# A log-sum-exp scan that is bound by its DMA engines: an opening store, and a part of one tile stored through GpSimd's queue

## Chip, cores, metric

One Trainium2 (trn2) chip, one core. The metric is the time on the device in microseconds (us); lower is better.

## The reference

```python
# x: (8, 4096, 2048) float32; a running log-sum-exp along axis 1
out[:, 0, :] = x[:, 0, :]
for t in range(1, S):
    mx = np.maximum(out[:, t - 1, :], x[:, t, :])
    out[:, t, :] = mx + np.log(np.exp(out[:, t - 1, :] - mx) + np.exp(x[:, t, :] - mx))
```

## The kernel before

The kernel takes 64 tiles of 128 partitions x 4 rows x 2048 columns (4 MB each), in six buffers. SP loads a tile; ScalarE (ACT) takes Exp; VectorE (DVE) adds the four rows of each partition; TensorE makes the sums over the partitions before; VectorE adds them; ACT takes Ln and stores the tile. Every load and store covers all 128 partitions. The parts that matter here:

```python
def parts(n):                                   # pieces in which a tile is stored
    m = 2 if n == NT - 1 else 1
    return [slice(k * R // m, (k + 1) * R // m) for k in range(m)]
...
for rows, c in ((slice(0, 2), top), (slice(2, R), loaded[0])):   # first tile, ahead of the block
    c(nc.sync.dma_start(out=ti[0][:, rows, :], in_=x_v[0][:, rows, :]), 16)
...
# SP: loads
for n in range(1, NT):
    i = n % NI
    if n >= NI:
        sp.wait_ge(stored[i].s, n // NI * 16)   # the store that frees the buffer
    loaded[i](sp.dma_start(out=ti[i][:], in_=x_v[n]), 16)
...
# ACT, in ln(n), second half of the columns
stored[n % NI](act.dma_start(out=o_v[n][:, rows, :], in_=t[:, rows, :]), 16)
...
# after the block
for c in stored:
    nc.sync.wait_ge(c.s, c.n)
```

The softmax here doesn't subtract the row's maximum and nothing guards it: scores larger than these inputs give would overflow.

Of the kernel before, what the change touches and what calls it, by code (L numbers as in the profile page):

```python
# [8 lines left out]
@with_exitstack  # L9
def kernel(  # L10
    ctx: ExitStack,
    tc: tile.TileContext,
    x: bass.AP,
    out: bass.AP,
):











    nc = tc.nc
    f32 = mybir.dt.float32
    ACT = mybir.ActivationFunctionType
    nc.scalar.preload_act_table_set("natural_log_exp_and_others")  # L30

    B, S, D = x.shape
    P = 128
    R = 4
    NI = 6
    FD = 512
    HALF = D // 2
    NBLK = S // (P * R)
    NT = B * NBLK
    assert D == 4 * FD  # L40

    pool = ctx.enter_context(tc.tile_pool(name="io", bufs=1))
    psum = ctx.enter_context(tc.tile_pool(name="ps", bufs=1, space=bass.MemoryType.PSUM))
    before = pool.tile([P, P], f32, name="before", tag="before")
    last = pool.tile([P, P], f32, name="last", tag="last")
    ti = [pool.tile([P, R, D], f32, name=f"ti{i}", tag=f"ti{i}") for i in range(NI)]
    ps = [psum.tile([P, D], f32, name=f"ps{i}", tag=f"ps{i}") for i in range(2)]

    x_v = x.rearrange("b (k p r) d -> (b k) p r d", p=P, r=R)
    o_v = out.rearrange("b (k p r) d -> (b k) p r d", p=P, r=R)  # L50
    half = [slice(h * HALF, (h + 1) * HALF) for h in range(2)]

    def parts(n):

        m = 2 if n == NT - 1 else 1
        return [slice(k * R // m, (k + 1) * R // m) for k in range(m)]

    class Count:


        def __init__(self, name):
            self.s, self.n = tc.alloc_semaphore(name), 0

        def __call__(self, inst, by=1):
            inst.then_inc(self.s, by)
            self.n += by
            return self.n

    with tc.tile_critical():  # L69
        def counts(name, n):  # L70
            return [Count(f"{name}{i}") for i in range(n)]

        ones, shaped, logs, top, chain = (
            Count(s) for s in ("ones", "shaped", "logs", "top", "chain")
        )

        loaded, stored = counts("loaded", NI), counts("stored", NI)
        exps, sums, ahead, joined, carried = (
            counts(s, 2) for s in ("exps", "sums", "ahead", "joined", "carried")
        )  # L80


        for rows, c in ((slice(0, 2), top), (slice(2, R), loaded[0])):
            c(nc.sync.dma_start(out=ti[0][:, rows, :], in_=x_v[0][:, rows, :]), 16)  # L84

        with nc.Block() as block:  # L86

            @block.gpsimd
            def _(g):
                ones(g.memset(before[:], 1.0))  # L90
                ones(g.memset(last[:], 1.0))  # L91
                g.wait_ge(ones.s, ones.n)

                shaped(g.affine_select(  # L94
                    out=before[:], in_=before[:], compare_op=mybir.AluOpType.is_ge, fill=0.0,
                    base=-1, pattern=[[1, P]], channel_multiplier=-1,
                ))

                shaped(g.affine_select(  # L99
                    out=last[:], in_=last[:], compare_op=mybir.AluOpType.is_ge, fill=0.0,  # L100
                    base=-(P - 1), pattern=[[0, P]], channel_multiplier=1,
                ))

            @block.sync
            def _(sp):
                for n in range(1, NT):
                    i = n % NI
                    if n >= NI:
                        sp.wait_ge(stored[i].s, n // NI * 16)
                    loaded[i](sp.dma_start(out=ti[i][:], in_=x_v[n]), 16)  # L110

            @block.scalar
            def _(act):
                def exp(n):
                    t = ti[n % NI]
                    lo = 0
                    if n == 0:
                        lo = 2
                        act.activation(t[:, :lo], t[:, :lo], ACT.Exp)._wait_ge(top.s, 16)  # L119
                    for h in range(2):  # L120
                        a = act.activation(t[:, lo:, half[h]], t[:, lo:, half[h]], ACT.Exp)  # L121
                        if h == 0:
                            a._wait_ge(loaded[n % NI].s, (n // NI + 1) * 16)
                        exps[h](a)

                def ln(n):
                    t = ti[n % NI]
                    for h in range(2):
                        for rows in parts(n) if h else [slice(0, R)]:
                            logs(act.activation(  # L130
                                t[:, rows, half[h]], t[:, rows, half[h]], ACT.Ln
                            )._wait_ge(carried[h].s, n + 1))
                            if h:
                                act.wait_ge(logs.s, logs.n)
                                stored[n % NI](act.dma_start(  # L135
                                    out=o_v[n][:, rows, :], in_=t[:, rows, :]
                                ), 16)

                exp(0)
                for n in range(NT):  # L140
                    if n + 1 < NT:
                        exp(n + 1)
                    ln(n)

            @block.tensor
            def _(pe):
                def carry(n, h):

                    if n % NBLK == NBLK - 1:
                        pe.wait_ge(joined[h].s, n + 1)  # L150
                        pe.sem_inc(carried[h].s, 1)  # L151
                        return
                    for c in range(2 * h, 2 * h + 2):
                        sl = slice(c * FD, (c + 1) * FD)
                        m = pe.matmul(  # L155
                            ps[(n + 1) % 2][:, sl], last[:], ti[n % NI][:, R - 1, sl],
                            start=True, stop=False, skip_group_check=True,
                        )
                        if c == 2 * h:
                            m._wait_ge(joined[h].s, n + 1)  # L160
                    carried[h](m)

                def triangle(n, h):
                    for c in range(2 * h, 2 * h + 2):
                        sl = slice(c * FD, (c + 1) * FD)
                        m = pe.matmul(  # L166
                            ps[n % 2][:, sl], before[:], ti[n % NI][:, R - 1, sl],
                            start=n % NBLK == 0, stop=True, skip_group_check=True,
                        )
                        if c == 2 * h:  # L170
                            m._wait_ge(sums[h].s, n + 1)
                    ahead[h](m)

                pe.wait_ge(shaped.s, shaped.n)
                for n in range(NT):
                    for h in range(2):
                        triangle(n, h)
                    for h in range(2):
                        carry(n, h)

            @block.vector
            def _(dve):
                def local(n, h):
                    t, cols = ti[n % NI], half[h]
                    for r in range(1, R):
                        a = dve.tensor_add(t[:, r, cols], t[:, r - 1, cols], t[:, r, cols])  # L186
                        if r == 1:
                            a._wait_ge(exps[h].s, n + 1)
                        else:
                            a._wait_ge(chain.s, chain.n)  # L190
                        (chain if r < R - 1 else sums[h])(a)

                def join(n, h):
                    t, cols = ti[n % NI], half[h]
                    joined[h](dve.tensor_add(  # L195
                        t[:, :, cols], t[:, :, cols],
                        ps[n % 2][:, cols].unsqueeze(1).to_broadcast([P, R, HALF]),
                    )._wait_ge(ahead[h].s, n + 1))

                for n in range(NT):  # L200
                    for h in range(2):
                        local(n, h)
                    for h in range(2):
                        join(n, h)

        for c in stored:
            nc.sync.wait_ge(c.s, c.n)


# [28 lines left out]
```

## Time and profile before

| | before |
|---|---|
| time, median of six runs | 1250.51 us (1250.36 to 1250.60) |
| bytes moved | 268.44 MB in, 268.44 MB out |
| mean rate over the span | 430 GB/s |
| busy: VectorE, ScalarE, TensorE | 82%, 73%, 52% |
| last landing of a store | 1246.77 us after the start |
| end of the span | 1248.83 us |

The kernel is bound by its DMA engines; the lines that show it stand in the prediction. A useful habit for such a kernel is to look at the sixteen landings of one transfer, one per engine: the last of them ends the transfer. For the last store before the change they lie between 1243.30 and 1246.77 us, and their mean is 1244.67.

### The profile page before, as it was taken

The page shows a single profiled execution, that of the slowest core. Times are in us where ns is not written, and L with a number is a line of the kernel's source. Part 1 is how long each engine was busy: PE and PEld are TensorE (multiplying, and loading weights), DVE is VectorE, ACT ScalarE, POOL GpSimd, SP SyncE. Part 2 cuts the span into 40 slices and gives each one's busy share as a digit, 9 for nine tenths or more (in the row PEclk, how much of TensorE's full clock was granted, in tenths as well). Part 3 has the DMA queues.
Part 4 walks back from the last instruction along what each step waited for, and adds up shares of the span by engine and source line. Part 5 has one row for each costly group of instructions (what it writes and reads, how often), then busy time and mean ns, then how long its engine had stood idle before and what let it go on. Part 6 is the DMA issues. An engine that isn't in the chain of part 4 may idle for free.

```text
span 1248.8 us, 2916 instructions
## 1 busy us (share of the span) xinstructions
PE 645.1 (52%) x960; PEld 213.4 (17%) x960; DVE 1022.3 (82%) x512; ACT 907.5 (73%) x259; POOL 1.1 (0%) x8
## 2 busy tenths in 40 slices
PE   2655456553556444655465544555545564455551
PEld 0211112111112111211111111111111121111110
DVE  5999978778787787887878878778787787877873
ACT  5987866867768677686776866867768677686773
POOL 0000000000000000000000000000000000000000
PEclk9899788787887868777678786787767878778776
DMA  9999999999999999999999999999999999999998
GB/s 403 420 431 431 430 437 436 427 434 432 437 435 426 435 432 437 433 428 435 431 437 433 430 435 430 437 431 432 436 430 436 432 432 435 431 436 432 431 435 361
DMA packets 18735, 537.06 MB, mean 430 GB/s; under 512 B 2080, under 2 KB 2080, under 8 KB 2080
## 3 DMA queue, kind: packets, MB, share of 16 engines
q1 hardware_dynamic: 9360, 268.44, 49.9%
q10 hardware_dynamic: 9360, 268.44, 49.8%
q8 instruction: 7, 0.11, 0.0%
q14 instruction: 8, 0.07, 0.0%
HBM read 268.44 MB, written 268.44 MB: 430 GB/s over the span
## 4 chain that ended last, share of the span: by engine, by line
DMA 80%; ACT 14%; DVE 4%; PE 1%; DVEq 0%; issue 0%; SPq 0%; ACTq 0%; PEldq 0%
DMA out_dram<-ti 41%; DMA ti<-in_x_dram 38%; ACT ti L130 7%; ACT ti L121 7%; DVE ti L195 2%; DVE ti L186 1%; PE ps L166 1%; DVEq L86 0%; PE ps L155 0%; SPq L84 0%; ACTq L135 0%; PEldq L151 0%; SPq L233 0%; SPq L69 0%
## 5 line engine op out<-in xcount | busy, mean ns | idle before, releaser
L121 ACT ACTIVATE ti<-ti 128x4096 f32<-128x4096 f32 (+1 forms) x128 | 452.5, 3582 | 308.2 <-DMA ti<-in_x_dram 306.0
L186 DVE TENSOR_TENSOR ti<-ti 128x1024 f32<-128x1024 f32 x384 | 464.6, 1224 | 196.6 <-ACT ti L121 187.9
L195 DVE TENSOR_TENSOR ti<-ti,ps 128x4096 f32<-128x4096 f32 x128 | 560.0, 4416 | 9.0 <-PE ps L166 8.8
L166 PE MATMUL ps<-ti,before 128*128 128x512 f32 x512 | 373.2, 879 | 347.1 <-DVE ti L186 347.0
L130 ACT ACTIVATE ti<-ti 128x4096 f32<-128x4096 f32 x129 | 455.8, 3576 | 9.5 <-PE ps L155 6.6
L155 PE MATMUL ps<-ti,last 128*128 128x512 f32 x448 | 271.9, 738 | 228.9 <-DVE ti L195 228.9
L166 PEld LDWEIGHTS ps<-ti,before 128*128 128x128 f32 x512 | 127.5, 276 | 607.4 <-DVE ti L186 503.2
L155 PEld LDWEIGHTS ps<-ti,last 128*128 128x128 f32 x448 | 85.9, 212 | 399.5 <-DVE ti L195 332.8
L119 ACT ACTIVATE ti<-ti 128x4096 f32<-128x4096 f32 x1 | 3.6, 3616 | 6.3 <-DMA ti<-in_x_dram 6.3
L30 ACT ACT_TABLE_LOAD x1 | 1.3, 1283 | 0.8 <-PEq L222 0.8
L94 POOL TENSOR_SCALAR_AFFINE_SELECT before<-before 128x128 f32<-128x128 f32 x1 | 0.3, 292 | 0.1
L99 POOL TENSOR_SCALAR_AFFINE_SELECT last<-last 128x128 f32<-128x128 f32 x1 | 0.3, 292 | 0.0
L90 POOL MEMSET before<- 128x128 f32 x1 | 0.2, 204 | 0.5 <-SPq L69 0.5
L91 POOL MEMSET last<- 128x128 f32 x1 | 0.2, 204 | 0.0
L222 POOL MEMSET const-bfloat16-1.0<- 128x1 bf16 x1 | 0.1, 101 | 0.0
L222 POOL MEMSET const-uint8-127<- 128x1 uint8 x1 | 0.1, 101 | 0.0
L222 POOL MEMSET const-float32-0.0<- 128x1 f32 x1 | 0.1, 98 | 0.3 <-issue 0.3
L222 POOL MEMSET const-float32-1.0<- 128x1 f32 x1 | 0.1, 98 | 0.0
## 6 DMA issues: line engine op xcount, KB each, us to landing
ti<-in_x_dram SPq DMA_DIRECT2D x63, 4096.0 KB, 38.5
out_dram<-ti ACTq DMA_DIRECT2D x63, 4096.0 KB, 44.0
ti<-in_x_dram SPq DMA_DIRECT2D x2, 2048.0 KB, 9.6
out_dram<-ti ACTq DMA_DIRECT2D x2, 2048.0 KB, 13.2
```

The lines of the kernel that those rows point to most:

```text
L30: nc.scalar.preload_act_table_set("natural_log_exp_and_others")
L90: ones(g.memset(before[:], 1.0))
L94: shaped(g.affine_select(out=before[:], in_=before[:], compare_op=mybir.AluOpType.is_ge, fill=0.0, base=-1, pattern=[[1, P]], channel_mult ...
L99: shaped(g.affine_select(out=last[:], in_=last[:], compare_op=mybir.AluOpType.is_ge, fill=0.0, base=-(P - 1), pattern=[[0, P]], channel_mu ...
L119: act.activation(t[:, :lo], t[:, :lo], ACT.Exp)._wait_ge(top.s, 16)
L121: a = act.activation(t[:, lo:, half[h]], t[:, lo:, half[h]], ACT.Exp)
L130: logs(act.activation(t[:, rows, half[h]], t[:, rows, half[h]], ACT.Ln)._wait_ge(carried[h].s, n + 1))
L155: m = pe.matmul(ps[(n + 1) % 2][:, sl], last[:], ti[n % NI][:, R - 1, sl], start=True, stop=False, skip_group_check=True,)
L166: m = pe.matmul(ps[n % 2][:, sl], before[:], ti[n % NI][:, R - 1, sl], start=n % NBLK == 0, stop=True, skip_group_check=True,)
L186: a = dve.tensor_add(t[:, r, cols], t[:, r - 1, cols], t[:, r, cols])
L195: joined[h](dve.tensor_add(t[:, :, cols], t[:, :, cols], ps[n % 2][:, cols].unsqueeze(1).to_broadcast([P, R, HALF]),)._wait_ge(ahead[h].s, ...
L222: nc = _bacc.Bacc("TRN2", target_bir_lowering=False, num_devices=1)
```

## The change

The intent: the store queue is opened at the start, so that the first real store doesn't pay for it; the engines are to end together, by having the fifth DMA engine skip a part of tile 40; and the end of the program is to be shorter. Cut to its core:

```diff
+        if n == NT - 1:
+            return [slice(0, 1), slice(1, 2), slice(2, R)]
+        return [slice(0, 2), slice(2, R)] if n == VIA else [slice(0, R)]
+    VIA, PASS = 40, 120
 ...
-    with tc.tile_critical():
+    with tc.tile_critical(no_gpsimd_drain=True):
 ...
+    # ACT, first thing: the opening store
+    warm(act.dma_start(out=o_v[0][0:16, 0, 0:1], in_=nc.const_aps.tensor(0.0, [16, 1], f32)), 16)
 ...
+    own = slice(0, P)
+    if n == VIA and rows.start == 0:
+        share.add(act)
+        own = slice(PASS, P)                    # ACT keeps 8 partitions
-    stored[n % NI](act.dma_start(out=o_v[n][:, rows, :], in_=t[:, rows, :]), 16)
+    stored[n % NI](act.dma_start(out=o_v[n][own, rows, :], in_=t[own, rows, :]), 16)
 ...
+    # SP, before load 46
+    if n - NI == VIA:
+        sp.wait_ge(passed.s, 16)
 ...
+    # GpSimd
+    aimed(g.dma_start(out=spare[0:5, 16:32], in_=spare[0:5, 0:16]), 16)   # "aims" the next one
+    aimed.now(g)
+    share.now(g)
+    rows = parts(VIA)[0]                        # rows 0 and 1
+    passed(g.dma_start(out=o_v[VIA][0:PASS, rows, :], in_=ti[VIA % NI][0:PASS, rows, :]), 16)
+    passed.now(g)
+    # then it sets most semaphores back by hand; SP does so for the stores, inside the block
-        for c in stored:
-            nc.sync.wait_ge(c.s, c.n)
```

More of the change, by code (lines that the diff above doesn't have):

```diff
@@ L45 @@
     last = pool.tile([P, P], f32, name="last", tag="last")
+    spare = pool.tile([8, 32], f32, name="spare", tag="spare")
     ti = [pool.tile([P, R, D], f32, name=f"ti{i}", tag=f"ti{i}") for i in range(NI)]
@@ L53, in parts, with __init__ @@
     def parts(n):
-        m = 2 if n == NT - 1 else 1
-        return [slice(k * R // m, (k + 1) * R // m) for k in range(m)]
+        if n == NT - 1:
+            return [slice(0, 1), slice(1, 2), slice(2, R)]
+        return [slice(0, 2), slice(2, R)] if n == VIA else [slice(0, R)]
+    VIA, PASS = 40, 120
+    every = []
     class Count:
-        def __init__(self, name):
-            self.s, self.n = tc.alloc_semaphore(name), 0
+        def __init__(self, name, alloc=nc.alloc_semaphore):
+            self.s, self.n = alloc(name), 0
+            if alloc == nc.alloc_semaphore:
+                every.append(self)
         def __call__(self, inst, by=1):
@@ L66, in __call__, with add, now, settle @@
             self.n += by
-            return self.n
-    with tc.tile_critical():
+        def add(self, engine):
+            engine.sem_inc(self.s, 1)
+            self.n += 1
+        def now(self, engine):
+            engine.wait_ge(self.s, self.n)
+        def settle(self, engine):
+            if self.n:
+                engine.add_instruction(mybir.InstEventSemaphore(
+                    name=f"I-{nc.next_id()}", engine=engine.engine, ins=[], outs=[],
+                    sync_info=mybir.SyncInfo(
+                        on_wait=[mybir.SyncWait(
+                            sync_type="semaphore", id=self.s.num, ant_name=self.s.name,
+                            wait_mode="sem-ge-imm", wait_value=self.n,
+                        )],
+                        on_update=[mybir.SyncUpdate(
+                            sync_type="semaphore", id=self.s.num, ant_name=self.s.name,
+                            update_mode="sem-sub-imm", update_value=self.n,
+                        )],
+                    ),
+                ))
+    with tc.tile_critical(no_gpsimd_drain=True):
         def counts(name, n):
             return [Count(f"{name}{i}") for i in range(n)]
-        ones, shaped, logs, top, chain = (
-            Count(s) for s in ("ones", "shaped", "logs", "top", "chain")
+        ones, shaped, logs, top, chain, warm, share, over = (
+            Count(s) for s in ("ones", "shaped", "logs", "top", "chain", "warm", "share", "over")
         )
+        aimed, passed = (Count(s, tc.alloc_semaphore) for s in ("aimed", "passed"))
         loaded, stored = counts("loaded", NI), counts("stored", NI)
@@ L80 @@
         )
-        for rows, c in ((slice(0, 2), top), (slice(2, R), loaded[0])):
-            c(nc.sync.dma_start(out=ti[0][:, rows, :], in_=x_v[0][:, rows, :]), 16)
-        with nc.Block() as block:
-            @block.gpsimd
-            def _(g):
-                ones(g.memset(before[:], 1.0))
-                ones(g.memset(last[:], 1.0))
-                g.wait_ge(ones.s, ones.n)
-                shaped(g.affine_select(
-                    out=before[:], in_=before[:], compare_op=mybir.AluOpType.is_ge, fill=0.0,
-                    base=-1, pattern=[[1, P]], channel_multiplier=-1,
-                ))
-                shaped(g.affine_select(
-                    out=last[:], in_=last[:], compare_op=mybir.AluOpType.is_ge, fill=0.0,
-                    base=-(P - 1), pattern=[[0, P]], channel_multiplier=1,
-                ))
-            @block.sync
-            def _(sp):
-                for n in range(1, NT):
-                    i = n % NI
-                    if n >= NI:
-                        sp.wait_ge(stored[i].s, n // NI * 16)
-                    loaded[i](sp.dma_start(out=ti[i][:], in_=x_v[n]), 16)
+        with nc.Block(no_gpsimd_drain=True) as block:
             @block.scalar
             def _(act):
+                with nc.allow_non_contiguous_dma(reason="one element per DMA engine"):
+                    warm(act.dma_start(
+                        out=o_v[0][0:16, 0, 0:1], in_=nc.const_aps.tensor(0.0, [16, 1], f32)
+                    ), 16)
                 def exp(n):
@@ L133, in ln @@
                             if h:
-                                act.wait_ge(logs.s, logs.n)
+                                logs.now(act)
+                                own = slice(0, P)
+                                if n == VIA and rows.start == 0:
+                                    share.add(act)
+                                    own = slice(PASS, P)
                                 stored[n % NI](act.dma_start(
-                                    out=o_v[n][:, rows, :], in_=t[:, rows, :]
+                                    out=o_v[n][own, rows, :], in_=t[own, rows, :]
                                 ), 16)
                 exp(0)
+                warm.now(act)
                 for n in range(NT):
@@ L143, in _ @@
                     ln(n)
+                over.add(act)
+            @block.sync
+            def _(sp):
+                for rows, c in ((slice(0, 2), top), (slice(2, R), loaded[0])):
+                    c(sp.dma_start(out=ti[0][:, rows, :], in_=x_v[0][:, rows, :]), 16)
+                for n in range(1, NT):
+                    i = n % NI
+                    if n >= NI:
+                        sp.wait_ge(stored[i].s, 16 * sum(len(parts(m)) for m in range(i, n, NI)))
+                        if n - NI == VIA:
+                            sp.wait_ge(passed.s, 16)
+                    loaded[i](sp.dma_start(out=ti[i][:], in_=x_v[n]), 16)
+                for n in range(NT - NI, NT):
+                    stored[n % NI].settle(sp)
             @block.tensor
@@ L150, in carry @@
                         pe.wait_ge(joined[h].s, n + 1)
-                        pe.sem_inc(carried[h].s, 1)
+                        carried[h].add(pe)
                         return
@@ L172, in triangle @@
                     ahead[h](m)
-                pe.wait_ge(shaped.s, shaped.n)
+                pe.wait_ge(shaped.s, 2)
                 for n in range(NT):
@@ L179, in _ @@
                         carry(n, h)
+                over.add(pe)
             @block.vector
@@ L204, in _ @@
                         join(n, h)
-        for c in stored:
-            nc.sync.wait_ge(c.s, c.n)
+                over.add(dve)
+            @block.gpsimd
+            def _(g):
+                ones(g.memset(before[:], 1.0))
+                ones(g.memset(last[:], 1.0))
+                ones.now(g)
+                shaped(g.affine_select(
+                    out=before[:], in_=before[:], compare_op=mybir.AluOpType.is_ge, fill=0.0,
+                    base=-1, pattern=[[1, P]], channel_multiplier=-1,
+                ))
+                shaped(g.affine_select(
+                    out=last[:], in_=last[:], compare_op=mybir.AluOpType.is_ge, fill=0.0,
+                    base=-(P - 1), pattern=[[0, P]], channel_multiplier=1,
+                ))
+                ones(g.memset(spare[:], 0.0))
+                ones.now(g)
+                aimed(g.dma_start(out=spare[0:5, 16:32], in_=spare[0:5, 0:16]), 16)
+                aimed.now(g)
+                share.now(g)
+                rows = parts(VIA)[0]
+                passed(g.dma_start(
+                    out=o_v[VIA][0:PASS, rows, :], in_=ti[VIA % NI][0:PASS, rows, :]
+                ), 16)
+                passed.now(g)
+                over.now(g)
+                for c in every:
+                    if c not in stored:
+                        c.settle(g)
 _INS = ['x']
```

## The prediction

> **What bounds the kernel now.** I read the page from the top: the slices of the span, then the queues, then the chain.
>
> ```profile
> DMA  9999999999999999999999999999999999999998
> GB/s 403 420 431 431 430 437 436 427 434 432 437 435 426 435 432 437 433 428 435 431 437 433 430 435 430 437 431 432 436 430 436 432 432 435 431 436 432 431 435 361
> ...
> q1 hardware_dynamic: 9360, 268.44, 49.9%
> q10 hardware_dynamic: 9360, 268.44, 49.8%
> q8 instruction: 7, 0.11, 0.0%
> q14 instruction: 8, 0.07, 0.0%
> ...
> DMA 80%; ACT 14%; DVE 4%; PE 1%; DVEq 0%; issue 0%; SPq 0%; ACTq 0%; PEldq 0%
> ```
>
> The 16 DMA engines are full from the second slice to the last but one; the two data queues take 49.9 + 49.8% of their time. The program must move 537 MB whatever it does, and the change moves the same bytes. So only four things can shorten it: the start (403 and 420 GB/s in the first two slices), the last slice (361), an uneven load of the 16 engines, and what lies outside the transfers. The waits say that compute never starves the queues:
>
> ```profile
> SPq L110 <- DMA out_dram<-ti: 1145.3, 58, 58.2
> ...
> ACT ti L121 <- DMA ti<-in_x_dram: 306.0, 59, 6.0
> ```
>
> A load waits for the store that frees its buffer, and is issued 19.35 us apart (the distance of two loads in the trace). It lands 38.5 us later, so about one full load is always queued ahead of it, and the engines never see an empty ring. An engine that is late therefore stays late, and the slowest of the 16 sets the end. Stretches show it:
>
> ```profile
> 0.00:31.00 31.00, 8.64 (x12) 2.99 (x12) 15.46 (x8) 16.65 (x7) 1.08 (x8) 1.00 0.96 405
> 31.00:62.00 31.00, 20.26 (x32) 6.67 (x32) 30.51 (x17) 28.03 (x9) 0.00 (x0) 0.83 1.00 421
> ...
> 1235.00:1247.00 12.00, 0.00 (x0) 0.00 (x0) 0.00 (x0) 0.00 (x0) 0.00 (x0) 0.50 0.77 328
> ```
>
> The last two columns are DMA share and GB/s. From 1235 on no compute engine works any more. The last landing is at 1246.77, the span's end at 1248.83, and the measured time 1250.37.
>
> **The sixteen engines one by one.** The trace names no engine for a packet, but an engine starts its next packet 3 ns before the last one's modelled end, and each takes eight packets of every transfer and then one 4-byte semaphore write. With those two rules the packets fall into 16 chains of exactly 520 packets per queue. The ends of the last data packets: seven chains at 1242.96 to 1243.5, seven at 1244.4 to 1244.85, and **two stragglers at 1246.30 and 1246.29**. Why they differ:
> - One 16 KB fetch of instructions on q8 costs its chain about 1.35 us (the fetch, 0.95, and some 0.39 more on the packet after it). The seven fetches fall on seven chains: most of the middle group.
> - Straggler A gets four of the 8 KB fetches on q14 (at 103, 404, 715, 1025 us). Each takes 0.309 and lengthens the next packet by 0.54: 4 x 0.85 = 3.4 us, which is its lag over the fastest chain (3.34). No q8 fetch falls on it.
> - Straggler B has no fetch at all. Its 32 KB packets take 1213 ns like everybody's until about 390 us; after that some 260 of them take about 5 to 20 ns more, 2.7 us in all. It is also the chain that starts last (2.79 us against 2.04).
>
> [...]q1 and q10 alternate packet by packet.
>
> **The change part by part.**
> 1. *Relief of the fifth engine.* Two rows of tile 40 are 16 KB per partition. Before, each engine stores 8 x 16 KB = 128 KB of them. After, fifteen engines store 8 partitions each, the fifth none, and the eight remaining partitions leave by ACT[...]. The fifth loses 128 - 16 = 112 KB; seven others gain 16 KB. At 1213 ns per 32 KB that is 3.5 x 1.213 = 4.25 us less and 0.61 us more. I take straggler A, with its constant 3.4 us of fetches, to be that fifth engine: a relief of 4.2 us is made for such a lag. Then A ends near 1242.1 and is out of the way. But B ends within 5 ns of A. If B drifts again, the last landing stays; if B's drift is of this execution alone, the end falls back to the middle group, 1246.30 - 1244.85 = 1.45 us, or less where one of that group gets the extra 0.61. I give both about half: **-0.7 us**.
> 2. *A third queue on fifteen engines.* [...]the fetches above stall the next packet by 0.25 to 0.54 us. Five engines pay it early for the aiming transfer, fifteen in mid-run. If each pays once and B among them, up to 0.85 us. Estimate **+0.3 us**.
> 3. *Opening store.* At 40.3 to 43 us, when the first store meets the loads, the next two packets of every chain take 1.4 to 2.1 us in place of 1.213; the excess is 0.67 to 1.04 us per chain, about 0.9. That is most of the 421 against 432 GB/s in that stretch: 31 x 11 / 432 = 0.8 us. If the cost is that of opening the store queue, sixteen single elements stored at the head take it while the first loads are still on their way (they start at 2.04 us, ACT can issue before SP's first at 1.02). If it belongs to the meeting of two streams, it comes back at 40 us. A little over half: **-0.5 us**.
> 4. *The end.* After the last landing the kernel before runs through three wait instructions (1246.79 to 1247.13), drains with GpSimd as the last to answer (the others by 1247.37, GpSimd at 1247.80), and then a barrier, a clear of a range of semaphores and another barrier until 1248.83. GpSimd's drain (0.43) goes, and two of the waits (0.15); the block's barrier, which ran hidden at 1232.7 to 1233.0, now follows the last landing (0.3). The semaphores set back by hand are done by GpSimd behind the last stores. **-0.3 us**.
> 5. *Off the path.* The Ln of tile 40 and of the last tile is cut into more pieces: 2 x 1.91 against 3.57 us, some 0.25 us of ScalarE each time, in a ScalarE that is 73% busy and waits 5.2 us per tile for loads. The last stores are issued at 1229.98 and 1232.31 but queue until 1237 and 1242; three pieces in place of two change nothing. GpSimd's share is asked for near 793.5 us. Beside the two other queues its eight 16 KB packets per engine take 8 x (0.61 + 2 x 1.21) = 24 us, estimated; load 46, which needs that buffer, was issued at 839.45. So the new wait of SP ends before the old one.
>
> Sum: -0.7 + 0.3 - 0.5 - 0.3 = -1.2, so 1250.4 - 1.2 = **1249.2 us**.
>
> **The rivals.**
> - *The other straggler holds the end.* For it: 1246.29 against 1246.30. Against: its drift starts suddenly at 390 us, so it may depend on how the engines are in step. Then relief is worth nothing, and with the third queue's cost the time is 1250 to 1250.8; with B among the seven that get 16 KB more, 1251.
> - *The fifth engine is not A.* Then A remains and gets the third queue's cost on top: 1250.5 to 1251.3. If it is B, A remains just as well.
> - *Everything works.* Opening store -0.9, relief -1.45, end -0.3, third queue hidden: 1247.7.
> - *GpSimd's transfer is late*[...], and load 46 starves the loads. Its slack is about 20 us plus one queued load of 19 us, and stores would fill the engines meanwhile; I see no way to more than 1 us.
>
> **Range and chances.** The best case is about 1247.7 and the bad ones about 1251.2; with a little room for the good side, since the author kept the change, 1247.2 to 1251.0 for 8 in 10. Two per cent are 25 us, twenty times what any part moves; only a failure such as GpSimd's transfer stalling all queues could do that. Faster 0.01, within 0.98, slower 0.01.
>
> **What would show it.** Relief: among sixteen chains one ends about 1 us ahead of the fastest others; the last landing is B's or of the middle group. Opening store: the second slice near 430 GB/s and no packets of 1.4 to 2.1 us at 40 to 43 us; if they are still there, that step is wrong. Third queue: long packets right after the first ones of GpSimd's queue near 794 us. The end: span's end less last landing about 1.8 in place of 2.06 us. A wait of SP for GpSimd's transfer, or a gap of loads near 839 us, would make the prediction wrong upwards; a straggler group that ends before 1244 would make it wrong downwards.

What is cut from it, where the marks stand, are rules that no trace of this case shows, and the clauses that rested on them. The sum came to -0.7 + 0.3 - 0.5 - 0.3 = -1.2, so 1249.2 us. That the engine left out is the fifth is what the change intends, and that the fifth and seven others take ACT's 8 partitions was my assumption; the trace of before shows neither. Step 2's +0.3 is an estimate from the fetches alone, which lengthen the packet behind them by 0.25 to 0.54 us.

## The result

The changed kernel takes 1255.46 us (median of six, 1253.45 to 1258.54), the kernel before 1250.51: 5 us more, and a spread of 5 us where there was one of 0.24. The ratio is 1.004 (95% interval 1.0025 to 1.0055). Ratios here are the mean time of one kernel's runs over that of the other's of the same rounds, so not quite the ratio of the medians that I quote. Executions over 1.5% slower than the fastest of the same kernel are left out of the means. The prediction said 1249.2 with a range to 1251.0: wrong, in sign and in size.

The page of the changed kernel, with the lines that answer to the prediction's (DMA share and GB/s in 40 slices of 31.4 us; then the queues with packets, MB and share of 16 engines):

```profile
DMA  9999999999999999999999999999999999999997
GB/s 401 418 434 434 433 434 435 434 434 431 432 432 433 433 432 431 432 434 434 434 434 434 433 432 432 395 414 434 430 433 434 434 429 433 433 433 432 433 429 332
...
q1 hardware_dynamic: 9360, 268.44, 49.7%
q10 hardware_dynamic: 9552, 266.47, 49.3%
q0 software_dynamic: 176, 1.97, 0.6%
```

The first 25 slices are as before, 401 and 418 at the start included: the opening store has not mended the start. Then come 395 and 414 in the slices of 784 to 847 us, and 332 in place of 361 at the end. GpSimd's store (q0) is issued at 794.17 us, so the dip is its neighbourhood. 31.4 us x ((433 - 395) + (433 - 414)) / 433 = 4.1 us are lost there.

The stretch 800 to 830 us, before and after (us, busy time of the engines with counts in brackets, granted clock, DMA share, GB/s):

```profile
800.00:830.00 30.00, 16.51 (x23) 5.70 (x24) 23.54 (x15) 24.24 (x7) 0.00 (x0) 0.78 1.01 435
```
```profile
800.00:830.00 30.00, 12.08 (x20) 4.10 (x20) 17.11 (x9) 14.29 (x5) 0.00 (x0) 0.83 1.00 377
```

Look at the last two columns: the engines are busy all the time in both (share 1.00), and yet move 377 GB/s where they moved 435. So the engines don't stand idle for want of work; **the packets themselves take longer**. The packets of the trace say which. A 16 KB packet takes 611 ns and a 32 KB packet 1213 ns when undisturbed. Between 785 and 860 us I add up what all packets take beyond that, in engine-us (microseconds summed over the sixteen DMA engines):

| excess over 785 to 860 us | before | after |
|---|---|---|
| loads (q1; they write SBUF) | 0.1 | 1.6 |
| ACT's stores (q10; they read SBUF) | 0.1 | 22.0 |
| GpSimd's store (q0; it reads SBUF) | - | 39.3 |

Some of GpSimd's packets took 2.5 us in place of 0.61. Here stores suffer, loads hardly. Spread over 16 engines, 62.8 engine-us are 3.9 us.

The rest is balance. Before, the last load's sixteen parts land within 3.3 us and are complete at 1207.5 us; after, within 10.3 us, and complete at 1211.1. The last tile's compute needs all sixteen, so its last store is issued at 1236.4 us in place of 1232.3, and the engines that are ahead have nothing to do: from 1150 us to the last landing the 16 engines are idle for 72 engine-us in place of 34 (what the packets' durations leave over), which is 2.4 us more for each. 3.9 + 2.4 = 6.3, and the last landing of the profiled run moved from 1246.77 to 1253.05, by 6.3 us. (That execution took 1256.8 us, a long one of the six.)

The wait that I had watched for didn't come. SP's waits:

```profile
SPq L176 <- DMA out_dram<-ti: 1153.2, 58, 57.8
SPq L90 <- SPq L90: 75.2, 6, 19.1
```

The first line is the wait for stores as before; no line names GpSimd's store. Load 46, which waits for both parts of tile 40's store, was issued at 847.40 us, when ACT's part had landed (847.38); GpSimd's had landed some 19 us earlier, 33.8 us after its issue:

```profile
out_dram<-ti ACTq DMA_DIRECT2D x62, 4096.0 KB, 44.1
out_dram<-ti POOLq DMA_DIRECT2D x1, 1920.0 KB, 33.8
```

### The profile page after: what moved, and what is told of

Same layout as the page of the kernel before. It is cut to its first block, busy times and chain, and to the rows that moved or that the text cites. A ratio compares the mean times of both kernels' runs of the same rounds, so it can differ in the third digit from the quotient of the medians.

```text
span 1255.1 us, 2963 instructions
## 1 busy us (share of the span) xinstructions
PE 633.6 (50%) x960; PEld 210.7 (17%) x960; DVE 1022.5 (81%) x512; ACT 908.0 (72%) x261; POOL 2.3 (0%) x11
## 4 chain that ended last, share of the span: by engine, by line
DMA 79%; ACT 13%; DVE 4%; PE 1%; DVEq 1%; issue 0%; ACTq 0%; SPq 0%; PEldq 0%
DMA out_dram<-ti 42%; DMA ti<-in_x_dram 37%; ACT ti L144 7%; ACT ti L135 7%; DVE ti L231 2%; DVE ti L222 2%; PE ps L201 1%; DVEq L118 1%; PE ps L190 0%; ACTq L153 0%; SPq L169 0%; PEldq L80 0%; SPq L299 0%; SPq L104 0%
## 5 line engine op out<-in xcount | busy, mean ns | idle before, releaser
L144 ACT ACTIVATE ti<-ti 128x4096 f32<-128x4096 f32 (+2 forms) x131 | 456.2, 3524 | 10.4 <-PE ps L190 6.5
L190 PE MATMUL ps<-ti,last 128*128 128x512 f32 x448 | 261.1, 712 | 239.5 <-DVE ti L231 239.5
L133 ACT ACTIVATE ti<-ti 128x4096 f32<-128x4096 f32 x1 | 3.6, 3616 | 6.4 <-DMA ti<-in_x_dram 6.4
## 6 DMA issues: line engine op xcount, KB each, us to landing
out_dram<-ti POOLq DMA_DIRECT2D x1, 1920.0 KB, 33.8
```

Source lines behind the costliest of these rows:

```text
L133: act.activation(t[:, :lo], t[:, :lo], ACT.Exp)._wait_ge(top.s, 16)
L144: logs(act.activation(t[:, rows, half[h]], t[:, rows, half[h]], ACT.Ln)._wait_ge(carried[h].s, n + 1))
L190: m = pe.matmul(ps[(n + 1) % 2][:, sl], last[:], ti[n % NI][:, R - 1, sl], start=True, stop=False, skip_group_check=True,)
```

## The experiments

Eighteen kernels ran; the time is the median, and the kernel before stood at 1250.5 to 1250.6 (1251.3 in the last). "Excess" is the sum explained above, over the same 75 us. The results were correct except in one run, marked. Where an expectation shows a cut, it named a mechanism, or a rule by which partitions are dealt to engines, that no trace of this case shows.

### Which part of the change costs?

**no_share**: the changed kernel without GpSimd's work and without the cut of tile 40.

```diff
-    return [slice(0, 2), slice(2, R)] if n == VIA else [slice(0, R)]
+    return [slice(0, R)]
-    aimed(g.dma_start(...)); share.now(g); passed(g.dma_start(...)); passed.now(g)
```

> The changed kernel without GpSimd's transfer (and without the aiming one); the opening store, the last tile in three pieces and the new end stay. Theory (GpSimd's transfer costs the DMA engines time and upsets their balance): 1249.8 to 1250.6 us, no slices of 395 and 414 GB/s, the 16 landings of the last store within about 3.5 us. Rival (the head or the end costs): 1254 us or more. If the opening store gains what the prediction said, below 1249.8.

Measured: 1250.70 us, ratio 1.0001; excess 0.2; the last sixteen landings from 1243.98 to 1246.85. The loss is gone, so it belongs to GpSimd's work and the cut of tile 40. And what remains, opening store, three last pieces and the new end, gains nothing together.

**before_plus_share**: the kernel before with the aiming transfer and GpSimd's share alone.

```diff
+    aimed(...); share.now(g); passed(g.dma_start(out=o_v[VIA][0:120, 0:2, :], in_=ti[VIA % NI][0:120, 0:2, :]), 16)
```

> The kernel before with only the aiming transfer and GpSimd's share of tile 40. Theory: 1254 to 1257 us, with the dip to about 400 GB/s near 800 us. Rival (the loss needs the opening store or the new end): 1251 us or less.

Measured: 1257.46 us (1254.02 to 1258.66), excess 27.5, with 424 and 416 GB/s in the slices near 800 us. The share alone makes the loss.

**before_plus_opening**: the kernel before with the opening store alone.

> The kernel before with the opening store alone. From the trace of the run without share (excess at the first meeting of loads and stores 0.69 us per engine against 0.89): 1250.2 to 1250.7 us, not to be told from before. The prediction's step wanted 0.5 us less: 1250.0.

Measured: 1250.43 us, ratio 0.9999. Its first two slices:

```profile
GB/s 403 420 434 430 430 436 435 430 433 431 437 434 431 432 430 437 436 429 433 431 437 436 429 434 430 437 435 431 434 430 436 435 432 435 429 436 434 430 435 361
```

403 and 420, the figures of before.

**share_by_act**: the same cut (120 and 8 partitions of two rows, then the rest), all by ACT.

```diff
-    share.add(act)
+    stored[n % NI](act.dma_start(out=o_v[n][0:PASS, rows, :], in_=t[0:PASS, rows, :]), 16)
```

> The same cut of tile 40 into 120 and 8 partitions of two rows and the rest, but all by ACT's queue. Theory (it is GpSimd's queue): near the run without any share, 1250 to 1251 us. Rival (cut and uneven split over engines, the longer wait for the buffer): at least half of the 5 us, 1252.5 us or more.

Measured: 1252.42 us, between the two. Excess 12.8, and 8.7 of it lies on the eight packets of the 8-partition store, which took 1.07 to 2.25 us in place of 0.61; the 120 partitions had none to speak of (0.5 us from 793 to 830). So part of the cost is ACT's own 8 partitions. More on this run below.

### Is it GpSimd's queue?

**gp128**: GpSimd stores all 128 partitions of the two rows, ACT nothing of them.

```diff
-    VIA, PASS = 40, 120
+    VIA, PASS = 40, P
-    own = slice(PASS, P)
+    continue
```

> GpSimd stores all 128 partitions of the two rows, so 16 engines take 8 packets each and ACT none. Theory (every packet of GpSimd's queue costs its engine about 0.5 us beyond its bytes, 8 per engine): mean of the last 16 landings again about 4 us later than without share, time 1253.5 to 1257 us. Rival (leaving out the fifth engine is what costs): 1250 to 1251.5 us.

Measured: 1250.71 us, excess 0.2. My theory, a fixed cost of every GpSimd packet, falls at once: 128 such packets cost nothing, and not one of them took longer than 625 ns. The stretch:

```profile
800.00:830.00 30.00, 13.63 (x21) 4.03 (x20) 18.65 (x9) 17.62 (x5) 0.00 (x0) 0.73 1.00 432
```

### Is it the displaced engines?

New theory, a guess that no trace had shown: the engine left out moves the shares behind it to engines that read other partitions in a whole store, and the packets get longer for it. I took 5, 11 and 1 partitions sent ahead to move 11, 5 and 15 of the shares, and none sent ahead to move none; that too was a guess.

**no_aim**, **aim11**, **aim1**: no aiming transfer, or one of 11 or 1 partitions in place of 5.

```diff
-    aimed(g.dma_start(out=spare[0:5, 16:32], in_=spare[0:5, 0:16]), 16)
+    aimed(g.dma_start(out=spare[0:11, 16:32], in_=spare[0:11, 0:16]), 16)     # or 0:1, or nothing
```

> The changed kernel without the aiming transfer: [...] New theory ([...]128 partitions by GpSimd cost nothing and the 120 by ACT showed no long packets): no share is displaced, so almost no long packets between 795 and 830 us beyond those of the eight partitions; 1250.5 to 1252.5 us. Rival (any 120-partition transfer of GpSimd, or leaving one engine out, costs): 1254 us or more, packets as long as in the changed kernel.

> Aiming with 11 partitions in place of 5: [...] New theory: total excess of packets about 5/11 of the changed kernel's 63 us, some 25 to 35 us; time 1251.5 to 1254 us. Rival (displacement doesn't matter): as the changed kernel, 1254 to 1258 us.

> Aiming with 1 partition: [...] New theory: excess 15/11 of 63 us or more, 70 to 100 us; time 1255 us or more. Rival: as the changed kernel.

Measured: 1254.73, 1257.06 and 1255.42 us; excess 24.6, 27.3 and 30.7. There is no dose to be seen, and without any aiming the loss is there. This theory's forecasts fell too. But the runs didn't vary what they were meant to vary, as the next lines show: as far as the traces tell, the 120 partitions were dealt out the same way in all of them. So I take them as repeats, which tell the noise: five traces with this dealing (these three, the change, before_plus_share) have an excess of 24.6 to 62.8.

With the packets sorted into sixteen chains, one chain takes no data of GpSimd's store; in its place it shows eight empty 4-byte packets on q0, one per round. This is that chain in the changed kernel (start in ns, duration, queue, KB):

```
815953+1213 q10 32 | 817186+1213 q1 32 | 818395+611 q10 16 | 819002+1213 q1 32 | 820212+611 q10 16 | 820819+1213 q1 32 |
822028+611 q10 16 | 822635+1213 q1 32 | 823845+611 q10 16 | 824452+1213 q1 32 | 825661+611 q10 16 | 826268+1213 q1 32 |
827478+611 q10 16 | 828085+1213 q1 32 | 829294+611 q10 16 | 829901+1213 q1 32 | 831111+611 q10 16 | 831730+1213 q10 32
```

It takes eight 16 KB packets of q10, the other two rows, and no ninth: it is not among the eight engines that store ACT's 8 partitions. The same holds for no_aim, aim1 and before_plus_share. So **the engine left out takes none of ACT's 8 partitions**, where step 1 of the prediction gave it one; its number no trace tells. Fifteen engines have 8 packets each and one has 8 empty ones with 0, 1, 5 or 11 partitions sent ahead. The aiming transfers went to all sixteen engines as well: that of five partitions shows five 64-byte packets and eleven empty ones. In all these runs that chain is one without instruction fetches and, at 790 us, 0.45 to 0.65 us behind the first, never a straggler.

The trace of share_by_act is less disturbed and sorts better, though chains of like phase can still be taken for each other. The chain with the four 8 KB fetches (104, 404, 715, 1024 us) and the one that slows down by itself (packets some 10 ns long) are both among the eight that take a ninth packet. The last two chains end at 1248.43 and 1248.22 us. The change's 8 partitions thus go to just the two engines that needed relief.

### Is it what the store reads?

**hbm_source** (result wrong): GpSimd's transfer reads the input in HBM and not SBUF.

```diff
-    in_=ti[VIA % NI][0:PASS, rows, :]
+    in_=x_v[VIA][0:PASS, rows, :]
```

> Wrong result on purpose: GpSimd's transfer of the same shape, to the same place, with the same aiming reads the rows from the input in HBM and not from SBUF. New theory[...]: nearly no long packets, 1250.5 to 1252.5 us. Rival (GpSimd's packets on 15 displaced engines cost whatever they read; HBM or the queue): excess as in the changed kernel, 1254 us or more.

Measured: 1251.45 us, excess 1.9 (1.6 of it on ACT's 8 partitions). It fits a cost of reading SBUF. It doesn't prove it, since the edit changed a second thing: from HBM the 120 rows were dealt to all sixteen engines, seven or eight packets each.

### Is it the number of partitions, or which ones?

**gp64_four_rows**: GpSimd stores four rows of partitions 0 to 63, ACT those of 64 to 127. **gp112**: `PASS` = 112.

> GpSimd stores four rows of partitions 0 to 63 (4 packets of 32 KB on each of 16 engines), ACT those of 64 to 127: the same bytes as the 128 partitions of two rows, no engine left out, no empty packets. The aiming can't matter any more (the three aimings all left out one engine that takes no part of the eight-partition store). Theory[...]: long packets among SBUF-reading ones, excess 20 us or more, little in the loads; 1252 to 1258 us. Rival (the engine left out, or GpSimd's empty packets on it, upsets the rest): no excess, 1250.5 to 1251.5 us.

> GpSimd stores 112 partitions of two rows (7 each on 16 engines if they are dealt out evenly), ACT the other 16. [...]excess 20 us or more, 1252.5 to 1258 us. Rival (engine left out): only the sixteen of ACT long, under 1251.5 us.

Measured: 1266.58 us, far more than I expected, with an excess of 114, and 1253.68 us with 21.8 (4.9 of it on ACT's sixteen). Both deal packets to all sixteen engines, so no engine left out and no empty packets are needed for the loss. That rival is out.

**act_halves**: no GpSimd at all; ACT stores tile 40 as partitions 0 to 63 and then 64 to 127.

```diff
+    stored[n % NI](act.dma_start(out=o_v[n][0:64, rows, :], in_=t[0:64, rows, :]), 16)
+    own = slice(64, P)
```

> No GpSimd transfer; ACT stores tile 40 as partitions 0 to 63 and then 64 to 127. Theory[...]: long packets here too, 32 KB ones of ACT's queue[...]: excess 5 to 40 us, 1250.7 to 1254 us. Rival (only GpSimd's queue does it): no long packets, as the run without share.

Measured: 1257.37 us (1253.27 to 1259.3), more than I expected, excess 33.5. Its slices:

```profile
GB/s 400 417 434 431 434 434 434 434 432 434 433 433 434 432 434 434 434 434 430 432 434 432 434 434 433 434 402 434 433 432 433 434 433 433 431 434 433 434 428 284
```

402 in the 27th slice, and 284 in the last. One 4 MB store of 64, cut in two halves by partitions, costs 6.8 us. GpSimd's queue isn't needed for the loss.

**one_row**: the change with one row in place of two.

> The change with one row in place of two: 120 packets of 8 KB on GpSimd's queue. [...]a cost by bytes: excess of the changed kernels' 25 to 63 us about halved, 1251.5 to 1254 us. If the cost is by packets: as the changed kernel, 1254 to 1258 us.

Measured: 1251.22 us, excess 2.4. Half the bytes cost a tenth or less; I had expected half. There may be a threshold; with one run between none is shown.

**extra_0_64** and **extra_32_96**: all stores stay whole with ACT; GpSimd makes one extra transfer of four rows of 64 partitions, to a place that the last tile's store overwrites later. The two differ only in the partitions.

```diff
-    out=o_v[VIA][0:PASS, rows, :], in_=ti[VIA % NI][0:PASS, rows, :]
+    out=o_v[NT - 1][0:64, rows, :], in_=ti[VIA % NI][0:64, rows, :]       # or 32:96 and 32:96
```

> An extra transfer by GpSimd of 2.1 MB from partitions 0 to 63 of tile 40, written where the last tile's store later overwrites it; all stores of the program stay whole with ACT. 2.1 MB at 435 GB/s are 4.8 us. [...]GpSimd's packets far longer than 1.213 us, excess 60 us or more; 1258 to 1268 us. Rival (the count of partitions or what stays for ACT did it): excess equal to that of extra_32_96.

> The same with partitions 32 to 95.[...] no long packets (excess under 3 us); 1255 to 1256.5 us, the 4.8 us of the bytes alone. Rival: as extra_0_64.

Why the first set of partitions was expected to cost more than the second, here and in the next two runs, no trace had shown. Read it as a guess that these four runs test.

Measured: 1268.03 us (four runs; a fifth, slow, took 1288.6) and 1255.96 us; excess 67.5 and 13.2. The stretch of each, extra_0_64 first:

```profile
800.00:830.00 30.00, 14.27 (x21) 4.53 (x20) 18.71 (x9) 14.14 (x4) 0.00 (x0) 0.80 1.01 376
```
```profile
800.00:830.00 30.00, 11.82 (x20) 4.08 (x20) 18.17 (x10) 18.67 (x6) 0.00 (x0) 0.84 1.01 424
```

376 against 424 GB/s for the same bytes, count, queue and destination's kind. Of its 5.5 us, extra_32_96 spends 4.8 on its bytes. But its excess should have been under 3, and was 13, so the guess missed there.

**extra2_0_64** and **extra2_32_96**: the same with two rows, so with the 16 KB packets of the change.

> The extra transfer by GpSimd with two rows: 1.05 MB, four 16 KB packets per engine, partitions 0 to 63[...]. The bytes alone cost 2.4 us, so 1252.9 to 1253.2 without conflicts. [...]excess 8 to 40 us among packets that read SBUF; 1253.5 to 1258 us. Rival (only big packets suffer): excess under 2 us.

> The same with partitions 32 to 95[...]. [...]excess under 2 us, 1252.7 to 1253.5 us. Rival (any transfer of 64 partitions): excess as in extra2_0_64.

Measured: 1255.15 and 1253.36 us (before 1251.29 with a spread of 3.6, so times say less here); excess 13.9 and 3.3, where I had hoped for under 2. Which partitions are read seems to decide most of it at this size too: the factor between the two, 4.2, and that of the pair before, 5.1, are more than the 2.5 by which the five like traces differ, but each rests on one trace.

**gp_tile**: GpSimd stores the whole of tile 40.

> GpSimd stores the whole of tile 40, 128 partitions of four rows, ACT none of it. [...]no long packets, 1250.5 to 1252 us, though GpSimd's packets are as long as in the 64-partition runs. Rival (32 KB packets on a third queue cost): excess of tens of us, 1254 us or more.

Measured: 1266.29 us, the median of five runs (1264.52 to 1281.91; a sixth, slow, took 1288.71), a clear miss. Its profiled execution counts as slow, so I don't explain the loss from that trace; the fast runs have it as well, ratio 1.017. Why a whole tile by GpSimd costs 14 us and more, and half a tile (gp128) nothing, stays open. The rival that its expectation names, a cost of 32 KB packets on a third queue, stands.

## Why the prediction was wrong, point by point

**The cause.** The runs show when packets get longer, and not by what mechanism. The cases side by side, with what was read in pieces beside the whole stores:

| case | partitions, rows, queue | excess, engine-us |
|---|---|---|
| gp128 | all 128, two rows, GpSimd | 0.2 |
| 120 partitions in share_by_act | 0 to 119, two rows, ACT | 0.5 |
| one_row | 0 to 119, one row, GpSimd | 2.4 |
| extra2_32_96 | 32 to 95, two rows, GpSimd | 3.3 |
| ACT's 8 partitions in share_by_act | 120 to 127, two rows, ACT | 8.7 on 8 packets |
| extra_32_96 | 32 to 95, four rows, GpSimd | 13.2 |
| extra2_0_64 | 0 to 63, two rows, GpSimd | 13.9 |
| the change and its aimings, before_plus_share | 0 to 119, two rows, GpSimd | 25 to 63 |
| act_halves | 0 to 63, then 64 to 127, four rows, ACT | 33.5 |
| extra_0_64 | 0 to 63, four rows, GpSimd | 67 |
| gp64_four_rows | 0 to 63, four rows, GpSimd | 114 |

What is shown: in the change the loss comes with the cut by partitions (the same two rows of all 128 cost nothing, gp128); a cut makes it without GpSimd too (act_halves); the long packets are mostly those that read SBUF (61 of 63 engine-us in the change, but 11.5 of gp64_four_rows' 114 and 7.7 of act_halves' 33.5 lie on loads); and partitions 0 to 63 have four to five times the excess of partitions 32 to 95. What isn't shown: why it matters which partitions are read, for the trace doesn't tell which engine reads which partition. And a second cause isn't ruled out: extra_32_96 still had 13, and gp_tile, with all 128 partitions, still lost 14 us and more; both have 32 KB packets on a third queue.

**The steps of the prediction.**

- *What bounds the kernel*: right. The engines are full and the slowest ends it. The two stragglers were there again without the share: in no_share two chains end at 1246.38 and 1246.37 us, 1.5 us behind the next. One of them has four 8 KB instruction fetches (0.85 us each in the trace of before: 0.31 for the fetch and 0.54 more on the packet behind it); why the packets of the other get some 10 ns longer is open.
- *Step 1, relief of the fifth engine, -0.7 us*: this step failed. It took for granted that leaving one engine out costs the others nothing but the 16 KB of ACT's 8 partitions, and that the engine left out is straggler A. Neither holds. Long packets cost 25 to 63 engine-us, 1.5 to 3.9 us for each engine, and then the engines waited for one another; the engine left out had no lag to be relieved of; and both stragglers were among the eight that got the 0.61 us more (as share_by_act sorts). The aiming transfer made no difference that the traces show: with 5 partitions it went to all sixteen engines, as five 64-byte packets and eleven empty ones, and without it 15 engines took 8 packets each just the same. That the engine left out would be the fifth I had taken from the change's intent.
- *Step 2, a third queue, +0.3 us*: it names the right place and the wrong size and reason. In gp128 the third queue costs nothing: 1250.71 us against 1250.70 without it.
- *Step 3, opening store, -0.5 us*: wrong. At the first meeting of loads and stores (38 to 48 us) the excess per engine is 0.98 us in no_share, 0.88 in gp128 and 0.91 in before_plus_opening, which open the queue, and 0.89 in before and 0.91 in before_plus_share, which don't. (The 0.69 in before_plus_opening's expectation left out packets that start at 39.1 us.) The changed kernel's own trace has 0.60, but the time of before_plus_opening shows no gain. The cost belongs mainly to the meeting of the two streams, the second reading that the step had offered.
- *Step 4, the end, -0.3 us*: wrong. From the last landing to the end of the span it is 2.05 us after and 2.06 before. The block's barrier now comes after the last landing, and two ranges of semaphores are cleared in place of one. And the 0.43 us weren't GpSimd's: in the trace of before its semaphore rises at 1247.22, and it is SP that stands still from 1247.40 to 1247.80. Such a pause of SP's is there after the change (1253.38 to 1253.81) and in no_share (1247.26 to 1247.68) as well.
- *Step 5, off the path*: right. The store by GpSimd landed after 33.8 us, later than the 24 that I had worked out (28.0 in gp128, where no packet was long) but ahead of ACT's, and SP never waited for it.
- *The rivals*: "the other straggler holds the end" was too small: in no_share both hold it, and nothing is lost. "The fifth engine is not A" had the right premise, that no late engine was spared, but its 1250.5 to 1251.3 knew nothing of long packets. None of the rivals made other queues' packets slower. The sentence that a stall of all queues would take a failure of GpSimd's transfer came nearest.

The reason for the error in one sentence: I treated the sixteen engines as sixteen independent servers and counted bytes per server, where one transfer can make the packets of the others longer (ACT's stores took 22.0 engine-us more in the 75 us around GpSimd's); by what, is not shown.

No version of these runs beats the kernel before. no_share, before_plus_opening and gp128 equal it, and so does one_row within the noise (interval 0.9993 to 1.0017); the other runs with right results are slower, by 0.2 to 1.7%.

## What to carry to other kernels

In a kernel like this one, with full DMA engines, cut transfers by what lies within a partition (here rows) and keep all 128 partitions: two rows of 128 partitions by GpSimd cost nothing, while one store cut into partitions 0 to 63 and 64 to 127 cost 6.8 us. That isn't enough by itself: four rows of 128 partitions by GpSimd cost 14 us and more. Before a transfer is meant to spare one engine, look in the trace which engine it spares, and whether that one was late. And a DMA share of 1.00 with falling GB/s, 435 to 377 here, meant that packets had become longer; add up their durations by queue before any wait is blamed.
